# A two-block network on one Trainium2 core: modulation products placed in block one and the first FFN, high parts of weights on ScalarE, a scheduler that knows a shared port

## The chip, the core and the metric

The kernel runs on one core of a Trainium2 chip. Five engines work side by side: TensorE (PE in the profile, its weight loads PEld), VectorE (DVE), ScalarE (ACT), GpSimd (POOL) and SyncE (SP), which here only issues DMAs. The metric is the time of one execution on the device in microseconds, the median of several runs.

## The reference, cut to what matters

A token sequence of 512 x 1024 goes through two blocks in float32. Block one has two layers: a wide projection `w_in`, five kinds of attention, a gated merge, an output projection. Block two has two layers of a mixer (layer 0: convolution and mLSTM; layer 1: latent attention, MLA) and a gated convolutional FFN. In block two each layer's inputs are modulated:

```python
mod_l = jnp.split((jax.nn.silu(c) @ ada_w[layer] + ada_b[layer])[:, None, :], 6, axis=-1)
mod_c = jnp.split(jax.nn.silu(c_ctx) @ ada_w[layer] + ada_b[layer], 6, axis=-1)
h_lat = _modulate(xl, mod_l[0], mod_l[1])          # rms(x) * (1 + scale) + shift
...
xl = xl + mod_l[2] * y_lat
xl = xl + mod_l[5] * _conv_ffn(_modulate(xl, mod_l[3], mod_l[4]), ...)
```

`c` and `c_ctx` are inputs, so the modulation vectors (six vectors of 1024 for each layer and each of the two conditions) depend on nothing that the network computes. They can be made at any time before their first use.

## The kernel before, in words

Every float32 matmul is made of three: an operand is split into a high part in the type float32r and a low part, the difference, and high x high, high x low and low x high are added in PSUM (`mm3`). Activations are split when they are made. Weights are split by `wtile`: a DMA brings up to 128 x 1024 numbers into one of four `wraw` buffers, a cast writes `whi`, a subtraction writes `wlo`; both have four buffers too. In `split` the cast may go to VectorE or ScalarE (`ev`), the subtraction to VectorE or GpSimd (`tt`).

The modulation vectors don't use TensorE. `ada(l, chunks)` takes, for each chunk, four tiles of 128 rows of the transposed `ada_w` (one 512 KB DMA each, into a `wraw` buffer) and makes for each tile and condition one fused multiply-and-sum on VectorE: `ada_junk` is its unused product, `mod` the sum. A chunk is half of a vector of 1024, so a layer has twelve: 0 to 3 are shift and scale of its mixer, 4 and 5 the mixer's gate, 6 to 9 shift and scale of its FFN, 10 and 11 the FFN's gate. Layer 1 needs only its first four for the context too. That makes 160 products. Before, they stand so: layer 0's chunks 0 to 5 in block one, three in each of its layers (48 products); its other six and layer 1's chunk 0 in block two's mixer (56); chunks 1 to 6 in the first FFN (36); 7 to 11 in the MLA (20).

The order of work is written by `Plan`. Instructions are first recorded, each with a priority (its place in the code, or one that `spread` and `mix` assign between two others) and with one or more engines that could run it. `flush` then simulates the engines with a cost for each operation, gives each instruction to an engine, and emits all in the order of the simulated starts. Stages that end with a flush: block one (both layers), the mixer, the first FFN, the MLA, the second FFN.

The mixer (`mixer`) runs, in rough order: the gate projections; a depthwise convolution over 31 taps in four channel groups, each tap one instruction on VectorE that adds into `u` (120 of them, and four that begin a group), reading the padded input `apad`, of which there are two buffers; the projections of q, k, v; scans over gates; 24 units of four heads (matrices `dm`, products `ps_nd`, results `hs`); a norm of `u`; the output projection. The FFNs (`ffn`) and the output projections are long rows of matmuls. At the end of a layer of block one the last gated merge runs (`zm`: `ps_mm`, `gt`, `ps_br`, `acc`), then the merged sum is split (`mh`, `ml`) and projected with `w_out`.

Line numbers of the profile: nearly all recorded instructions have line 119, the recorder; L679 is the cast in `ev`, L695 the operation in `tt`, L690 and L691 `scale_rows`.

Of the kernel before, what the change touches and what calls it, by code (L numbers as in the profile page):

```python
# [93 lines left out]
class Op:  # L94
    __slots__ = ("i", "prio", "alts", "left", "ready", "succ", "tiles", "first", "table", "nbytes", "best", "end", "vis", "done", "nm", "why", "cols", "preds")
# [37 lines left out]
class Plan:  # L133
# [4 lines left out]
    def __init__(self, tc):  # L138
        self.tc, self.real = tc, tc.nc
        r = tc.nc  # L140
        self.tensor = PlannedEngine(self, "t", r.tensor)
        self.vector = PlannedEngine(self, "v", r.vector)
        self.scalar = PlannedEngine(self, "s", r.scalar)
        self.gpsimd = PlannedEngine(self, "g", r.gpsimd)
        self.sync = PlannedEngine(self, "y", r.sync)
        self.tile_of = {}
        self.seen = set()
        self.ops = []
        self.hist = {}
        self.kept = set()  # L150
        self.into = ()
        self.free = {e: 0.0 for e in "tsvgy"}
        self.dma_free = 0.0
        self.table = None
        self.ham = [-1, False, 0.0]
        self.released = {}
# [67 lines left out]

    def add(self, alts, name, a, k):
# [9 lines left out]
        if alts[0][0] == "t":  # L235
            dt = ins[0].dtype
            big = name != "transpose" and dt == F32
            op.cols = (4 if big else 1) * self.size(outs[0]) * ins[0].ap[0][1] / P
        op.left, op.ready, op.succ, op.done = 0, 0.0, [], False
# [131 lines left out]
    def flush(self):  # L371
# [51 lines left out]
        dma_free, table, ham = self.dma_free, self.table, self.ham  # L423
# [45 lines left out]
        while remaining:  # L469
# [22 lines left out]
            while ready[e]:  # L492
# [15 lines left out]
                if len(o.alts) > 1:  # L508
                    mine = t + o.alts[j][2] + self.LAT[e]
                    other = min((max(free[a[0]], t) + queue(a[0], p) + a[2] + self.LAT[a[0]], a[0])  # L510
                                for a in o.alts if a[0] != e)
                    if other[0] < mine:
                        heapq.heappush(pend[e], (max(free[other[1]], t + 60.0), p, i, j))
                        continue
# [35 lines left out]
            end = t + cost  # L550
# [97 lines left out]
class Net:  # L648
# [93 lines left out]
    def wtile(self, src, m, n):  # L742
# [7 lines left out]
        self.split(hv, lv, rv, m * n)  # L750
# [170 lines left out]
class BlockOne:  # L921
# [707 lines left out]
    def layer(self, l, xT):  # L1629
# [25 lines left out]
        for i, nm in enumerate(seq):  # L1655
# [16 lines left out]
            if nm == "nsa":  # L1672
                plan.spread(self.topk, self.topk[0], a0)
        for _ in self.zm(BRANCHES.index(seq[-1]), h, ys[seq[-1]], acc, False):
            pass
# [9 lines left out]
        for d, ps in n.proj_T(self.I["w_out"][l], (mh, ml), slice(0, S), D):  # L1685
# [4 lines left out]
            if l == self.layers - 1:  # L1690
                self.sums_g.add(xT[:, d], self.gain_eps[:, d:d + 1])
        return xT
# [24 lines left out]
class BlockTwo:  # L1717
# [3 lines left out]
    def beside_one(self, l, i):  # L1721

        if (l, i) == (0, 0):
            self.vecs()
            self.ada_setup()
        elif i in (1, 2, 3):
            self.ada(0, [3 * l + i - 1])
# [154 lines left out]
    def run(self, xp, xT, layers=DEPTH):  # L1882
        n, nc, tc, I = self.n, self.nc, self.tc, self.I
        self.xp = xp
        with ExitStack() as ctx:
# [4 lines left out]
            with ExitStack() as c2:  # L1890
                wk, pp = n.plan.pool(c2, "b2m"), n.plan.pool(c2, "b2mp", PSUM)
                n.wk, n.nt2 = wk, 6
                a = len(n.plan.ops)
                xT, xc = self.mixer(xT, xc, h, wk, pp)
                b = len(n.plan.ops)
                self.ada(0, range(6, 12))
                n.plan.spread((b, len(n.plan.ops)), self.begun, 0.3 * a + 0.7 * b)
                self.ada(1, [0])
# [3 lines left out]
            h = self.ffn(0, h, xT, xc, lambda: self.ada(1, range(1, 6)),  # L1902
                         lambda: (self.ada(1, [6]), self.normed("h_mla", 1, 0, xT, xc), self.weights_mla())[1])
# [19 lines left out]
    def mixer(self, xT, xc, h, wk, pp):  # L1923
# [66 lines left out]
        for half in range(2):  # L1990
            o = 2048 + 264 * half
            for t, ps in n.proj(w[:, o:o + 264], h, 264, range(6)):
                if (half, t) == (0, 0):
                    first = len(n.plan.ops)
                if (half, t) == (0, 3):
                    n.plan.spread(late, first, len(n.plan.ops))
                    self.begun = len(n.plan.ops)
# [271 lines left out]
    def mla(self, h, xT):  # L2269
        n, nc, tc, I = self.n, self.nc, self.tc, self.I  # L2270
        LAT, CTX = self.LAT, self.CTX
        with ExitStack() as ctx:
# [191 lines left out]
            a = len(n.plan.ops)  # L2464
            self.ada(1, range(7, 11))
            n.plan.spread((a, len(n.plan.ops)), 0.5 * first + 0.5 * a, 0.1 * first + 0.9 * a)
            self.ada(1, [11])
# [61 lines left out]
```

## Time and profile before

| | |
|---|---|
| median of 3 runs | 3292.95 us (3288.82 to 3294.26) |
| profiled execution, its own time | 3291.55 us |
| its span, first to last instruction | 3289.8 us |
| mean granted clock of TensorE | 0.97 |
| DMA, mean over the span | 88 GB/s |

A busy time is the time in which an engine ran at least one instruction; the granted clock is the share of the full TensorE clock that the chip allowed (1.00 is 2.4 GHz). Stage borders in the span, read from the first and last instructions on tiles of each stage: block one's layers from 0 to 784 and from 784 to 1512 us, the mixer to 1936, the first FFN to 2500, the MLA to 2905, the second FFN and the output to the end.

### The profile page before, as it was taken

The page shows a single profiled execution, that of the slowest core. Times are in us where ns is not written, and L with a number is a line of the kernel's source. Part 1 is how long each engine was busy: PE and PEld are TensorE (multiplying, and loading weights), DVE is VectorE, ACT ScalarE, POOL GpSimd, SP SyncE. Part 2 cuts the span into 40 slices and gives each one's busy share as a digit, 9 for nine tenths or more (in the row PEclk, how much of TensorE's full clock was granted, in tenths as well). Part 3 has the DMA queues.
Part 4 walks back from the last instruction along what each step waited for, and adds up shares of the span by engine and source line. Part 5 has one row for each costly group of instructions (what it writes and reads, how often), then busy time and mean ns, then how long its engine had stood idle before and what let it go on. Part 6 is the DMA issues. An engine that isn't in the chain of part 4 may idle for free.

```text
span 3289.8 us, 43893 instructions
## 1 busy us (share of the span) xinstructions
PE 3081.8 (94%) x16488; PEld 2520.2 (77%) x16488; DVE 2391.8 (73%) x4762; ACT 1177.7 (36%) x2633; POOL 325.1 (10%) x281
## 2 busy tenths in 40 slices
PE   7999898998999898998896999999998999989999
PEld 6778776877777677877775878888887777668887
DVE  8787787656887887657999775555557878766654
ACT  5444434312434434314215631111115666631112
POOL 3110110011110100010221000000001101110000
PEclk8999899999999999999997999999999999989999
DMA  5442242234332332334222223223223102133322
GB/s 183 109 112 76 63 117 68 80 93 138 85 99 80 101 88 75 81 90 154 83 77 75 74 87 94 77 69 93 78 61 96 49 20 79 46 101 106 106 76 88
DMA packets 384813, 290.01 MB, mean 88 GB/s; under 512 B 13260, under 2 KB 353496, under 8 KB 384344
## 3 DMA queue, kind: packets, MB, share of 16 engines
q1 hardware_dynamic: 384600, 287.20, 30.1%
q8 instruction: 130, 2.13, 0.3%
q14 instruction: 83, 0.68, 0.1%
HBM read 268.67 MB, written 11.67 MB: 85 GB/s over the span
## 4 chain that ended last, share of the span: by engine, by line
PE 40%; DVE 10%; ACT 1%; issue 1%; DMA 1%; POOL 0%; ACTq 0%; DVEq 0%; POOLq 0%; SPq 0%
PE ps_mm L119 32%; DVE u L119 4%; PE ps_lg L119 2%; PE ps_tp L119 2%; PE ps_pv L119 2%; DVE ada_junk L119 1%; DVE y_mod L119 1%; PE ps_nd L119 1%; PE ps_st L119 1%; DVE dm L119 0%; DVE h_ffn L119 0%; DMA wraw<-in_ab_w_in_dram 0%; DVE sq L119 0%; DMA wraw<-in_ffn_w_in_dram 0%; DVE xT L119 0%
## 5 line engine op out<-in xcount | busy, mean ns | idle before, releaser
L119 PE MATMUL ps_mm<-h_ffn,whi 128*128 128x512 f32 (+1 forms) x2112 | 567.1, 357 | 14.7 <-DVE h_ffn L119 6.9
L679 DVE CAST whi<-wraw 128x1024 fp32r<-128x1024 f32 (+7 forms) x317 | 185.3, 585 | 453.8 <-PE ps_mm L119 441.5
L119 PEld LDWEIGHTS ps_mm<-h_ffn,whi 128*128 128x128 f32 x2112 | 375.9, 190 | 77.8 <-DVE h_ffn L119 10.4
L695 DVE TENSOR_TENSOR wlo<-wraw,whi 128x1024 fp32r<-128x1024 f32 (+4 forms) x359 | 379.1, 1056 | 21.3 <-ACT whi L679 9.5
L119 PE MATMUL ps_mm<-hh,wlo 128*128 128x512 f32 x960 | 389.2, 405 | 0.2 <-DVE wlo L695 0.2
L119 PE MATMUL ps_mm<-hl,whi 128*128 128x512 f32 x960 | 388.7, 405 | 0.0
L119 PE MATMUL ps_mm<-hh,whi 128*128 128x512 f32 x960 | 387.4, 403 | 0.0
L119 PE MATMUL ps_mm<-h_ffn,wlo 128*128 128x512 f32 (+1 forms) x1056 | 375.0, 355 | 0.0
L695 POOL TENSOR_TENSOR wlo<-wraw,whi 128x1024 fp32r<-128x1024 f32 (+6 forms) x102 | 187.4, 1839 | 1099.6 <-DVE whi L679 572.9
L119 DVE CUSTOM_DVE_ANT_0 ada_junk<-wraw,cond,cols 128x1024 bf16<-128x1024 f32 x160 | 216.8, 1355 | 19.3 <-DMA wraw<-in_ada_wT_dram 18.0
L119 PEld LDWEIGHTS ps_mm<-h_ffn,wlo 128*128 128x128 f32 x1056 | 200.6, 190 | 27.7
L679 ACT CAST whi<-wraw 128x1024 fp32r<-128x1024 f32 (+8 forms) x144 | 135.8, 944 | 227.1 <-PE ps_mm L119 161.2
L119 PEld LDWEIGHTS ps_mm<-hl,whi 128*128 128x128 f32 x960 | 182.7, 190 | 34.4
L119 PEld LDWEIGHTS ps_mm<-hh,wlo 128*128 128x128 f32 x960 | 182.4, 190 | 34.0 <-DVE wlo L695 0.6
L119 PEld LDWEIGHTS ps_mm<-hh,whi 128*128 128x128 f32 x960 | 182.6, 190 | 33.6 <-issue 1.2
L119 ACT ACTIVATE p<-ps_lg,mx 128x384 f32<-128x384 f32 (+3 forms) x288 | 155.7, 544 | 129.2 <-DVE mx L119 127.1
L119 PE MATMUL ps_mm<-fhi,wlo 128*128 128x512 f32 (+1 forms) x528 | 187.8, 357 | 0.0
L119 PE MATMUL ps_mm<-flo,whi 128*128 128x512 f32 (+1 forms) x528 | 187.1, 356 | 0.0
L119 PE MATMUL ps_mm<-fhi,whi 128*128 128x512 f32 (+1 forms) x528 | 186.8, 355 | 0.0
L679 ACT COPY gpad<-ps_mm 128x512 f32<-128x512 f32 (+1 forms) x63 | 32.8, 520 | 399.7 <-PE ps_mm L119 399.0
L119 DVE TENSOR_REDUCE mx<-ps_lg 128x1 f32<-128x384 f32 (+3 forms) x288 | 144.9, 505 | 28.6 <-PE ps_lg L119 26.6
L119 PE MATMUL ps_tp<-ident,p 128*128 128x128 f32 x768 | 133.3, 278 | 12.3 <-ACT p L691 5.9
(567 smaller groups left out, 6662.0 us busy)
## 6 DMA issues: line engine op xcount, KB each, us to landing
wraw<-in_w_in_dram SPq DMA_DIRECT2D x132, 512.0 KB
wraw<-in_ada_wT_dram SPq DMA_DIRECT2D x96, 512.0 KB
wraw<-in_ffn_w_in_dram SPq DMA_DIRECT2D x88, 512.0 KB
wraw<-in_ffn_w_out_dram SPq DMA_DIRECT2D x64, 256.0 KB
wraw<-in_w_branch_dram SPq DMA_DIRECT2D x20, 512.0 KB
wraw<-in_w_out_dram SPq DMA_DIRECT2D x16, 512.0 KB
wraw<-in_ab_w_in_dram SPq DMA_DIRECT2D x16, 512.0 KB
x_keep<-xT SPq DMA_DIRECT2D x3, 2048.0 KB
```

The lines of the kernel that those rows point to most:

```text
L119: return plan.add([(eng, lambda: fn(*a, **k))], name, a, k)
L679: self.plan.either("tensor_copy", {"v": lambda x: x.tensor_copy(out, in_), "s": lambda x: x.copy(out, in_)}, out, in_)
L695: f = lambda x: x.tensor_tensor(out, a, b, op=op)
```

## The change

Three things. The products: block one keeps three chunks beside the attention of each layer and gets three more at each layer's end (`fill(l, 5)`), so that all of layer 0's are made there; all twelve of layer 1's are recorded beside the first FFN; the mixer and the MLA have none. The cast of `wtile` is recorded for ScalarE alone; the subtraction may still go to VectorE or GpSimd. And `flush` simulates a port that VectorE and GpSimd share: an instruction with two large SBUF inputs, or a copy or scaling from SBUF to SBUF (`shares`), starts on one of the two engines only when the other's last such instruction has ended.

```diff
+    def shares(self, name, outs, ins):
+        big = [x for x in ins if self.size(x) > 1 and not self.in_psum(x)]
+        if len(big) > 1:
+            return True
+        return name in ("tensor_copy", "tensor_scalar", "scale") and len(big) == 1 and not self.in_psum(outs[0])
...
-                    mine = t + o.alts[j][2] + self.LAT[e]
-                    other = min((max(free[a[0]], t) + queue(a[0], p) + a[2] + self.LAT[a[0]], a[0])
+                    start = lambda x, at: max(at, port["v"]) if x == "g" else max(at, port["g"]) if x == "v" and o.port else at
+                    mine = start(e, t) + o.alts[j][2] + self.LAT[e]
+                    other = min((start(a[0], max(free[a[0]], t)) + queue(a[0], p) + a[2] + self.LAT[a[0]], a[0])
...
-            end = t + cost
+            begin = t
+            if e == "v" and o.port:
+                begin = max(t, port["g"])
+                port["v"] = begin + cost
+            elif e == "g" and o.port:
+                begin = max(t, port["v"])
+                port["g"] = begin + cost
+            end = begin + cost
...
-        self.split(hv, lv, rv, m * n)
+        self.nc.scalar.copy(hv, rv)
+        self.tt(lv, rv, hv.bitcast(F32), ALU.subtract, m * n)
...
+        if self.fill:
+            a = len(plan.ops)
+            self.fill(l, 5)
+            plan.spread((a, len(plan.ops)), tail + 0.1 * (a - tail), tail + 0.9 * (a - tail))
...
         elif i in (1, 2, 3):
-            self.ada(0, [3 * l + i - 1])
+            self.ada(0, [6 * l + i - 1])
+        elif i == 5:
+            self.ada(0, range(6 * l + 3, 6 * l + 6))
...
-                self.ada(0, range(6, 12))
-                n.plan.spread((b, len(n.plan.ops)), self.begun, 0.3 * a + 0.7 * b)
-                self.ada(1, [0])
...
-            h = self.ffn(0, h, xT, xc, lambda: self.ada(1, range(1, 6)),
-                         lambda: (self.ada(1, [6]), self.normed("h_mla", 1, 0, xT, xc), self.weights_mla())[1])
+            h = self.ffn(0, h, xT, xc, lambda: self.ada(1, range(12)),
+                         lambda: (self.normed("h_mla", 1, 0, xT, xc), self.weights_mla())[0])
...
-            self.ada(1, range(7, 11))
-            n.plan.spread((a, len(n.plan.ops)), 0.5 * first + 0.5 * a, 0.1 * first + 0.9 * a)
-            self.ada(1, [11])
```

How the built programs' orders differ at three places. First VectorE in the mixer, where the last taps (`u`) run before the heads' first `dm`; `ISA ada_junk` is a modulation product and `ISA mod` the instruction that reads out its sum. Before:

```order
L119 SCALAR_TENSOR_TENSOR u<-apad,cw,u 128x783 x6
L119 ISA ada_junk,mod<-wraw,cond,cols 128x1024
L119 ISA mod 128x1
L119 SCALAR_TENSOR_TENSOR u<-apad,cw,u 128x783
L119 ISA ada_junk,mod<-wraw,cond,cols 128x1024
L119 ISA mod 128x1
L119 SCALAR_TENSOR_TENSOR u<-apad,cw,u 128x783
L119 ISA ada_junk,mod<-wraw,cond,cols 128x1024
L119 ISA mod 128x1
L119 SCALAR_TENSOR_TENSOR u<-apad,cw,u 128x783
L119 TENSOR_TENSOR dm<-ps_mb,u 128x128
```

The same place in the changed kernel:

```order
L119 SCALAR_TENSOR_TENSOR u<-apad,cw,u 128x783
L119 TENSOR_SCALAR u<-apad,cw,cols 128x783
L119 SCALAR_TENSOR_TENSOR u<-apad,cw,u 128x783 x7
L712 TENSOR_TENSOR wlo<-wraw,whi 128x1024
L119 SCALAR_TENSOR_TENSOR u<-apad,cw,u 128x783 x12
L119 TENSOR_TENSOR dm<-ps_mb,u 128x128
```

No product stands among the taps any more; a low part that GpSimd or nobody made there stands among them now (three in this stretch).

Second VectorE near the end of block one's first layer, in the last gated merge. Before:

```order
L679 CAST whi<-wraw 128x1024
L695 TENSOR_TENSOR wlo<-wraw,whi 128x1024
L119 SCALAR_TENSOR_TENSOR gt<-gt,ps_br 128x512
L695 TENSOR_TENSOR acc<-acc,gt 128x512
L679 CAST whi<-wraw 128x1024
L695 TENSOR_TENSOR wlo<-wraw,whi 128x1024
```

In the changed kernel:

```order
L712 TENSOR_TENSOR wlo<-wraw,whi 128x1024
L119 SCALAR_TENSOR_TENSOR gt<-gt,ps_br 128x512
L712 TENSOR_TENSOR acc<-acc,gt 128x512
L119 ISA ada_junk,mod<-wraw,cond,cols 128x1024
L119 ISA mod 128x1
L119 ISA ada_junk,mod<-wraw,cond,cols 128x1024
L119 ISA mod 128x1
L712 TENSOR_TENSOR wlo<-wraw,whi 128x1024
```

The casts have left VectorE and pairs of products (one for each condition) have come in, 24 in each layer's end.

Third VectorE at the end of the MLA, where the sums of squares (`sq`) end and the modulated input of the second FFN (`y_mod`, `h_ffn`) begins. Before:

```order
L119 TENSOR_TENSOR sq<-sq 128x512
L119 ISA ada_junk,mod<-wraw,cond,cols 128x1024
L119 ISA mod 128x1
L119 ISA ada_junk,mod<-wraw,cond,cols 128x1024
L119 ISA mod 128x1
L119 ISA ada_junk,mod<-wraw,cond,cols 128x1024
L119 ISA mod 128x1
L119 SCALAR_TENSOR_TENSOR y_mod<-xT,mod,rstd 128x512 x3
```

In the changed kernel:

```order
L119 TENSOR_TENSOR sq<-sq 128x512
L119 SCALAR_TENSOR_TENSOR xT<-ps_mm,mod,xT 128x512
L119 TENSOR_TENSOR sq<-sq 128x512
L712 TENSOR_TENSOR wlo<-wraw,whi 128x1024
L119 SCALAR_TENSOR_TENSOR y_mod<-xT,mod,rstd 128x512 x3
```

Three products are gone there, and one of the four low parts that GpSimd made for the second FFN's first weights is on VectorE.

## Rows read from the trace of the kernel before

**Rows 1.** The page, part 1: busy us, share of the span, instructions.

```profile
PE 3081.8 (94%) x16488; PEld 2520.2 (77%) x16488; DVE 2391.8 (73%) x4762; ACT 1177.7 (36%) x2633; POOL 325.1 (10%) x281
```

**Rows 2.** Busy times by stage: window, engines' busy us (instructions), granted clock, DMA share, GB/s.

```profile
0.00:784.00 784.00, 721.48 (x3736) 585.51 (x3736) 587.26 (x1255) 305.50 (x642) 106.37 (x86) 0.97 0.36 102
784.00:1512.00 728.00, 677.50 (x3489) 547.01 (x3490) 547.33 (x1148) 278.36 (x585) 75.99 (x55) 0.98 0.32 90
1512.00:1936.00 424.00, 366.20 (x2103) 314.27 (x2101) 379.09 (x657) 163.68 (x426) 62.16 (x39) 0.91 0.31 95
1936.00:2500.00 564.00, 557.31 (x3176) 485.99 (x3176) 337.15 (x523) 105.34 (x159) 17.17 (x21) 1.00 0.28 84
2500.00:2905.00 405.00, 386.64 (x2371) 283.85 (x2370) 316.75 (x866) 251.43 (x716) 47.10 (x63) 0.98 0.17 52
2905.00:3290.00 385.00, 372.65 (x1616) 303.59 (x1616) 224.22 (x317) 73.43 (x109) 16.26 (x17) 0.97 0.32 94
```

**Rows 3.** The chain that ended last, shares of the span by line.

```profile
by line: PE ps_mm L119 31.9%; DVE u L119 4.2%; PE ps_lg L119 2.3%; PE ps_tp L119 2.0%; PE ps_pv L119 1.8%; issue 1.3%; DVE ada_junk L119 1.2%; DVE y_mod L119 0.8%; PE ps_nd L119 0.8%; PE ps_st L119 0.6%; DVE dm L119 0.4%; DVE h_ffn L119 0.4
```

**Rows 4.** Busy times in the mixer's stretches and at the second FFN's entry.

```profile
1563.00:1760.00 197.00, 163.31 (x844) 137.97 (x843) 196.70 (x228) 41.21 (x86) 37.15 (x15) 0.88 0.25 75
1760.00:1880.00 120.00, 106.16 (x684) 90.90 (x683) 100.33 (x294) 82.56 (x268) 17.46 (x10) 0.89 0.24 75
1880.00:1936.00 56.00, 54.09 (x309) 46.93 (x307) 37.37 (x58) 12.64 (x22) 0.00 (x0) 1.00 0.36 109
2895.00:2922.00 27.00, 14.10 (x26) 7.82 (x27) 24.98 (x27) 12.39 (x17) 10.97 (x10) 0.56 0.58 154
```

**Rows 5.** Busy times of `ada_junk` on VectorE alone, same columns: VectorE, clock, DMA.

```profile
1563.00:1760.00 197.00, 32.80 (x24) 0.88 0.25 75
1760.00:1880.00 120.00, 20.24 (x14) 0.89 0.24 75
1936.00:2500.00 564.00, 48.70 (x36) 1.00 0.28 84
```

**Rows 6.** Groups of TensorE, 1563 to 1760: busy us, mean ns, idle before and releaser.

```profile
L119 PE MATMUL ps_mm<-wlo,h 128*128 128x512 f32 x48 | 20.1, 420 | 3.3 <-POOL wlo L695 3.3
L119 PE MATMUL ps_nd<-mv,dm 128*128 128x129 f32 x12 | 3.7, 462 | 9.3 <-DVE dm L119 9.3
```

**Rows 7.** Groups of instructions over the whole span, shapes apart, same columns.

```profile
L119 DVE CUSTOM_DVE_ANT_0 ada_junk<-wraw,cond,cols 128x1024 bf16<-128x1024 f32 x160 | 216.8, 1355 | 19.3 <-DMA wraw<-in_ada_wT_dram 18.0
L679 DVE CAST whi<-wraw 128x1024 fp32r<-128x1024 f32 x188 | 130.6, 695 | 279.7 <-PE ps_mm L119 269.3 <-issue 5.2 <-DMA wraw<-in_w_in_dram 2.0
L679 ACT CAST whi<-wraw 128x1024 fp32r<-128x1024 f32 x108 | 113.2, 1049 | 187.5 <-PE ps_mm L119 126.6 <-DMA wraw<-in_ab_w_in_dram 41.2 <-DMA wraw<-in_w_in_dram 6.8
L695 DVE TENSOR_TENSOR wlo<-wraw,whi 128x1024 fp32r<-128x1024 f32 x245 | 298.6, 1219 | 13.4 <-ACT whi L679 4.3 <-PE ps_mm L119 0.3
L695 POOL TENSOR_TENSOR wlo<-wraw,whi 128x1024 fp32r<-128x1024 f32 x51 | 132.0, 2591 | 446.0 <-ACT whi L679 268.9 <-DVE whi L679 132.8 <-PE ps_tp L119 17.2
L119 DVE SCALAR_TENSOR_TENSOR u<-apad,cw,u 128x783 f32<-128x783 f32 x120 | 139.4, 1194 | 0.2
L119 PE MATMUL ps_mm<-hh,wlo 128*128 128x512 f32 x960 | 389.2, 405 | 0.2 <-DVE wlo L695 0.2
```

**Rows 8.** The tile `apad`, 1563 to 1760: durations in ns, smallest, median, largest.

```profile
L119 DVE SCALAR_TENSOR_TENSOR u<-apad,cw,u x120: 1017/1029/3191, 1564.4 to 1757.6; 128x783 f32<-128x783 f32 x120
```

**Rows 9.** Timeline at the second FFN's entry: start us, us, engine and instruction.

```profile
2907.62 7.88 POOL L695 TENSOR_TENSOR wlo<-wraw,whi 128x1024 fp32r<-128x1024 f32 x3 [5.31 <-ACT whi L679]
2910.46 5.59 DVE L119 SCALAR_TENSOR_TENSOR y_mod<-xT,mod,rstd 128x512 f32<-128x512 f32 x2
2915.98 0.74 DVE L119 SCALAR_TENSOR_TENSOR h_ffn<-y_mod,mod,h_ffn 128x512 fp32r<-128x512 f32 x1
```

**Rows 10.** Busy times in block one's attention and at its first layer's end.

```profile
300.00:360.00 60.00, 52.99 (x292) 43.31 (x292) 58.94 (x120) 34.41 (x51) 14.54 (x14) 0.99 0.25 73
580.00:735.00 155.00, 152.71 (x716) 122.66 (x715) 96.04 (x160) 39.77 (x85) 11.06 (x5) 1.00 0.31 84
```

More of the change, by code (lines that the diff above doesn't have):

```diff
@@ L94 @@
 class Op:
-    __slots__ = ("i", "prio", "alts", "left", "ready", "succ", "tiles", "first", "table", "nbytes", "best", "end", "vis", "done", "nm", "why", "cols", "preds")
+    __slots__ = ("i", "prio", "alts", "left", "ready", "succ", "tiles", "first", "table", "nbytes", "best", "end", "vis", "done", "nm", "why", "cols", "preds", "port")
 class PlannedPool:
@@ L155, in __init__ @@
         self.ham = [-1, False, 0.0]
+        self.port = {"v": 0.0, "g": 0.0}
         self.released = {}
@@ L238, in add @@
             op.cols = (4 if big else 1) * self.size(outs[0]) * ins[0].ap[0][1] / P
+        op.port = self.shares(name, outs, ins)
         op.left, op.ready, op.succ, op.done = 0, 0.0, [], False
@@ L422, in flush @@
         frontier = 0
-        dma_free, table, ham = self.dma_free, self.table, self.ham
+        dma_free, table, ham, port = self.dma_free, self.table, self.ham, self.port
         order = []
@@ L1673, in layer @@
                 plan.spread(self.topk, self.topk[0], a0)
+        tail = a0
         for _ in self.zm(BRANCHES.index(seq[-1]), h, ys[seq[-1]], acc, False):
@@ L1892, in run @@
                 n.wk, n.nt2 = wk, 6
-                a = len(n.plan.ops)
                 xT, xc = self.mixer(xT, xc, h, wk, pp)
-                b = len(n.plan.ops)
-                self.ada(0, range(6, 12))
-                n.plan.spread((b, len(n.plan.ops)), self.begun, 0.3 * a + 0.7 * b)
-                self.ada(1, [0])
                 h = self.normed("h_ffn", 0, 3, xT, xc)
@@ L1996, in mixer @@
                     n.plan.spread(late, first, len(n.plan.ops))
-                    self.begun = len(n.plan.ops)
                 nog = 264 if half == 0 else 248
@@ L2463, in mla @@
             out(3, y2)
-            a = len(n.plan.ops)
-            self.ada(1, range(7, 11))
-            n.plan.spread((a, len(n.plan.ops)), 0.5 * first + 0.5 * a, 0.1 * first + 0.9 * a)
-            self.ada(1, [11])
             h = self.normed("h_ffn", 1, 3, xT, None)
```

## Prediction, made before the changed kernel was run

> **What bounds the kernel now.** I read the view by engine first, then the same busy times cut at the stage borders, then the chain of work that ended last, and only then single instructions. TensorE (PE) is busy 94% of the span and VectorE (DVE) 73% [rows 1], and an average over six stages says little. Cut by stage [rows 2], the two FFNs leave TensorE almost nothing to win (557.31 us busy of 564, 372.65 of 385). The mixer of block two is the odd one: TensorE 366.20 of 424 us at a granted clock of 0.91, and VectorE 379.09 of 424, the only stage in which VectorE is busier than TensorE. Block one's two layers lie between: TensorE idles 62.5 and 50.5 us there.
>
> The chain says what that means [rows 3]: 4.2% of the span is the line of `u` (the convolution's taps) and 1.2%, some 39 us, is `ada_junk`, the modulation product. An instruction that only prepares numbers for later stands on the path that sets the end.
>
> Where it stands there is seen by cutting the mixer [rows 4]. From 1563 to 1760 VectorE is busy 196.70 of 197 us, while TensorE idles 34 us and is granted 0.88 of its clock. From 1760 to 1880 (the heads) VectorE has 100.33 of 120, TensorE 106.16 at 0.89, ScalarE (ACT) 82.56. From 1880 to 1936 TensorE has 54.09 of 56: bound by matmuls again. The products take 32.80 us (24 of them) of the first stretch and 20.24 us (14) of the second [rows 5]. TensorE's waits in the first name VectorE (9.3 us for `dm` alone), and 3.3 us go to a low part that GpSimd (POOL) makes [rows 6].
>
> **The change part by part.** *Products out of the mixer.* 56 of 160 leave the mixer and 20 leave the attention stage; 48 more go into the ends of block one's layers, 28 more into the first FFN. One takes 1.355 us on VectorE [rows 7].
>
> Taps' stretch, 1563 to 1760: VectorE is the bound, so the 32.80 us come off whole, unless something else is late. The order shows three low parts (`wlo`) among the taps on VectorE where there were none, 3 x 1.219 us [rows 7] = 3.7 us back. The casts don't count here: the mixer's were on ScalarE already but for six. Net 29; I take 28, for a POOL part more or less. The bounds: TensorE's 163.31 us in this stretch, at 0.88 of the clock, must still fit into 169. If neither its clock rises nor its other waits fall, little more than half is won, so -15. At the other end, the taps' excess over their median, 120 x (1194 - 1029) ns = 20 us [rows 7, 8], could go too: -48. What is late next: the scans behind the gates and GpSimd's low parts, which stay.
>
> Heads, 1760 to 1880: 20.24 us of products leave a VectorE that is 84% busy, beside a TensorE that idles 13.8 us. Nothing is won if TensorE and ScalarE pace the units, 20 if VectorE does. TensorE waits on `dm`, `hs` and `den` made by VectorE, and its idle time is the nearest measure: -12.
>
> Out-projection, 1880 to 1936: TensorE fills it [rows 4], so whatever leaves VectorE there was hidden: 0.
>
> *Entry of the second FFN.* From 2895 to 2922 TensorE has 14.10 of 27 us at 0.56 of the clock [rows 4]. VectorE there makes `y_mod` and `h_ffn`, 16 operations that take 0.74 us alone, but two `y_mod` took 5.59 us, just while three low parts ran on GpSimd for 7.88 us [rows 9]. Three products stand right before them. In the new order the products are gone, ScalarE casts these tiles ahead of `rstd`, and GpSimd's three (one less than before) can run earlier, beside the out-projection's sums. From 0 (they meet the `sq` sums instead) to -8 (twice that pair's excess of 4.1 us, for what else they held up); I take -5.
>
> *Products into block one's ends.* 24 more in each layer, 24 x 1.355 = 32.5 us. From 580 to 735 TensorE has 152.71 of 155, VectorE 96.04 [rows 10]. With the products it has 128.5, still 83%, less the casts that leave. The cover is the 59 us in which VectorE idles while TensorE multiplies; all 24 end before `mh` in the order, so the hand-over to the out-projection is not touched. Each product also brings a 512 KB DMA on SP's queue, through the four `wraw` slots that the weights use; DMA engines are 31% busy there. I take 0. The bound comes from 300 to 360 [rows 10]: VectorE at 58.94 of 60, TensorE at 52.99. If the ends became like that, 12% of 155 us in each layer would be lost, +36.
>
> *Products into the first FFN.* 36 become 64: 38 us more for a VectorE that idles 227 of 564 [rows 2]; 36 of them (48.70 us, [rows 5]) run there today beside a TensorE at 99%. 0. Without that cover they would cost the 38.
>
> *High parts on ScalarE.* All casts of weights on VectorE (the 188 widest alone are 130.6 us, 0.695 each) go to ScalarE, at 1.049 [rows 7]. ScalarE is busy 36% [rows 1]. The chain DMA, cast, subtract, matmul grows by 0.35 us for a tile, behind four buffers of each kind; TensorE's 960 matmuls with the low part in block one waited 0.2 us for it in all [rows 7]. So 0 on this side; the bound is 0.354 us for each of block one's 123 casts that move (by the order), +44. On the other side VectorE is relieved: in block one 123 casts leave, but the order puts 12 low parts, 11 `acc` sums and some smaller operations of GpSimd on it instead, about half of that. If a tenth of block one's 113 us of idle TensorE went, -11. I take 0 between.
>
> *The scheduler's port model* costs no instruction. It moves work from GpSimd (286 instructions in the program become 205) to VectorE, so its price is in the figures above.
>
> Sum: -28 - 12 - 5 = -45 us. The profiled execution took 3291.55 us, 1.75 more than its span, and lies 1.4 below the median of the runs, inside their spread. 3291.55 - 45 = 3246.5, so 3246.
>
> **Weighed against a rule.** The taps' median is 1.029 us and their longest 3.191 [rows 8]; a low part on GpSimd takes 2.591 [rows 7]: a tap can stand for most of one. The Trainium skill (SBUF — State Buffer, "Who interferes with whom") says that a DVE operation with two SBUF inputs and a GpSimd operation that reads SBUF take turns on one port pair, and that the one that comes second is blocked for the whole of the other. By that rule a scheduler that knows it could get rid of all of the excess; the sum would be -65 and the time 3226. The trace agrees with the blocking (taps of either 1.03 or up to 3.19 us); whether the plan avoids it is the first rival.
>
> **The rivals.** *The excess goes too.* If GpSimd's low parts in the mixer no longer meet the taps, the 20 us of excess go with the 45: 3226. For it: the planner now charges either engine for the other's time. Against: the order still has 16 low parts on GpSimd in the mixer (18 before), and the taps stand in a row with hardly anything between them that could run beside one. With a gain in block one as above, 3215.
>
> *TensorE takes VectorE's place in the mixer.* If the clock stays at 0.88 and the heads are paced by TensorE and ScalarE, -15, 0 and -5 are left: 3272. For it: 163.31 of 169 us would be nearly full. Against: the clock fell where TensorE starved (0.88 here against 1.00 in the first FFN).
>
> *Slower: the casts hold TensorE in block one.* There ScalarE also makes the exponentials and evictions on which attention waits; a cast of 1.049 us in front of one delays it. The 123 casts that move decide it: at 0.37 us of TensorE each the 45 us are gone, at 0.45 the kernel is slower by 10, 3302. For it: TensorE and VectorE are both near their limits in stretches like 300 to 360. Against: ScalarE has 34 of 60 us there, and the low parts were on time everywhere.
>
> *No change.* The taps could wait for matmuls instead of the products; then the mixer stays and only -5 is left, 3287. Against: VectorE idled 0.3 us in 197.
>
> **How the numbers follow.** Forecast (25 to 60 us faster) 0.60, own range 3231 to 3267; the excess goes too 0.12; TensorE takes the place 0.13; about no change 0.05; slower, through casts or the block's ends, 0.10. About 0.2%, 6.6 us, is what a measurement of this kernel can tell from no change: faster 0.85, same 0.05, slower 0.10. The range reaches from 3212 (just under the first rival with block one's gain) to 3282; that leaves out the slower cases, the unchanged one and the far end of the first rival, 0.18 to 0.2 in all.
>
> **What the profile would show.** Right: the mixer down from 424 to about 384 us, no `ada_junk` in it, the granted clock between the taps' start and the heads' end above 0.9, `ada_junk` gone from the chain or under 0.3%, the `u` share as it was; ends of block one still over 97% TensorE; first FFN 564 +- 3. Wrong: taps still without a gap and the stretch as long as before (something else fills VectorE); TensorE idle behind `whi` or `wlo` in block one (the casts); layers longer than 784 and 728 us with idle time before `ps_br` or `ps_mm` in their ends (the products or their DMAs).

## The result, and the profile after

The changed kernel took 3250.5 us (median of 4 runs, 3245.89 to 3252.26) where the kernel before took 3292.7: a ratio of 0.9871, 95% interval [0.9855, 0.9887]. The forecast was 3246. The profiled execution took 3249.24 us, its span 3247.5. The page of the changed kernel, by engine as in [rows 1]:

```profile
PE 3069.0 (95%) x16488; PEld 2518.3 (78%) x16488; DVE 2294.8 (71%) x4602; ACT 1396.0 (43%) x2874; POOL 204.4 (6%) x200
```

The busy times of the changed kernel by stage, cut where its own stages end, to be read against [rows 2]:

```profile
0.00:784.00 784.00, 722.83 (x3738) 588.30 (x3738) 589.95 (x1270) 366.33 (x708) 56.85 (x61) 0.97 0.39 112
784.00:1502.00 718.00, 675.14 (x3480) 549.06 (x3481) 540.97 (x1154) 326.36 (x634) 40.13 (x34) 0.97 0.35 97
1502.00:1900.00 398.00, 355.33 (x2110) 308.20 (x2108) 313.67 (x547) 170.46 (x435) 57.43 (x33) 0.94 0.22 64
1900.00:2469.00 569.00, 558.60 (x3177) 486.11 (x3178) 353.66 (x544) 153.75 (x210) 11.38 (x13) 1.00 0.35 105
2469.00:2872.00 403.00, 387.81 (x2370) 284.55 (x2369) 294.77 (x820) 260.07 (x730) 38.30 (x53) 0.98 0.12 35
2872.00:3247.00 375.00, 369.33 (x1616) 302.05 (x1616) 201.75 (x271) 119.01 (x161) 0.27 (x6) 0.99 0.30 87
```

The gain is where it was looked for. VectorE in the mixer went from 379.09 us to 313.67, so TensorE, with 355.33, is the busier engine there now as it is in the other stages, at a clock of 0.94 where it had 0.91. The two stretches of the mixer that were costed and the out-projection, as in [rows 4] (180, 94 and 65 us long):

```profile
1561.00:1741.00 180.00, 157.79 (x874) 137.37 (x872) 173.43 (x187) 44.44 (x94) 46.84 (x17) 0.92 0.19 53
1741.00:1835.00 94.00, 88.16 (x624) 76.69 (x625) 75.28 (x251) 75.42 (x253) 4.00 (x3) 0.98 0.08 24
1835.00:1900.00 65.00, 61.87 (x341) 52.75 (x339) 30.08 (x49) 20.37 (x35) 0.00 (x0) 0.97 0.24 76
```

For comparison between kernels, the stages below are cut at the same events in every trace: block one ends with the last matmul of its second output projection; the mixer (with its entry) and the MLA end with the first matmul on `h_ffn`; the first FFN ends with the first on `h_mla`; the last column is the second FFN and the output.

| us | block one | mixer | first FFN | MLA | second FFN, output |
|---|---|---|---|---|---|
| before | 1509.4 | 426.8 | 566.4 | 402.4 | 384.7 |
| after | 1502.4 | 398.0 | 568.2 | 403.8 | 375.1 |

So -7.0, -28.8, +1.8, +1.4 and -9.6: the span is 42.3 us shorter. Inside the mixer, from the first tap to the last, 195.0 us became 180.0; from there to the last `ps_nd` 113.1 became 93.3; and the wait between block one and the first matmul on the context, 5.9 us before, is 11.3 now.

The taps' stretch has 173.43 us of VectorE in 180, so VectorE is still its busiest engine, though no longer without a gap. Groups of VectorE and GpSimd there in the changed kernel, shapes apart (busy us, mean ns, idle before and releaser):

```profile
L119 DVE SCALAR_TENSOR_TENSOR u<-apad,cw,u 128x783 f32<-128x783 f32 x120 | 134.6, 1158 | 0.6
L119 DVE SCALAR_TENSOR_TENSOR og<-og,hg 128x512 f32<-128x512 f32 x6 | 8.3, 1392 | 0.0
L119 DVE TENSOR_TENSOR_SCAN b<-ones,lf 4x768 f32<-4x768 f32 x1 | 3.9, 3941 | 0.0
L119 DVE TENSOR_TENSOR_SCAN M<-ones,M,li 4x512 f32<-4x512 f32 x1 | 3.3, 3297 | 0.0
L712 POOL TENSOR_TENSOR wlo<-wraw,whi 128x1024 fp32r<-128x1024 f32 x15 | 45.5, 3044 | 127.1 <-ACT whi L119 127.1
```

and the two groups of the kernel before that they are read against, the sums `og` and GpSimd's wide low parts in its taps' stretch (the first two scans above took 1.737 and 1.274 us there):

```profile
L119 DVE SCALAR_TENSOR_TENSOR og<-og,hg 128x512 f32<-128x512 f32 x6 | 4.0, 685 | 0.0
L695 POOL TENSOR_TENSOR wlo<-wraw,whi 128x1024 fp32r<-128x1024 f32 x12 | 34.0, 2833 | 79.6 <-ACT whi L679 78.8 <-DVE u L119 0.8
```

The taps' excess did not go: 120 x (1158 - 1027) ns = 15.7 us is left of 20 (their smallest, median and longest below, as in [rows 8]), and `og` and two scans now have long ones too. GpSimd's wide low parts in the stretch rose from 12 to 15, from 34.0 to 45.5 us.

```profile
L119 DVE SCALAR_TENSOR_TENSOR u<-apad,cw,u x120: 1018/1027/3192, 1562.6 to 1740.1; 128x783 f32<-128x783 f32 x120
```

TensorE's longest wait in the stretch, by group, is a new one: a projection can't go on until `apad` of the next channel group is written (3.4 us before, at one place):

```profile
L119 PE MATMUL ps_mm<-whi,h 128*128 128x512 f32 x96 | 31.7, 411 | 12.5 <-DVE apad L119 12.5
```

At the second FFN's entry, the 27 us that answer to [rows 4] and one line of the timeline that answers to [rows 9]: TensorE has 20.38 us at 0.75 of the clock instead of 14.10 at 0.56, GpSimd 3.30 instead of 10.97, and three `y_mod` take 2.08 us where two took 5.59.

```profile
2862.00:2889.00 27.00, 20.38 (x67) 14.36 (x68) 20.07 (x26) 13.41 (x18) 3.30 (x8) 0.75 0.26 75
...
2870.84 2.08 DVE L119 SCALAR_TENSOR_TENSOR y_mod<-xT,mod,rstd 128x512 f32<-128x512 f32 x3 [4.12 <-ACT rstd L119]
```

### The profile page after: what moved, and what is told of

Same layout as the page of the kernel before. It is cut to its first block, busy times and chain, and to the rows that moved or that the text cites. A ratio compares the mean times of both kernels' runs of the same rounds, so it can differ in the third digit from the quotient of the medians.

```text
span 3247.5 us, 44054 instructions
## 1 busy us (share of the span) xinstructions
PE 3069.0 (95%) x16488; PEld 2518.3 (78%) x16488; DVE 2294.8 (71%) x4602; ACT 1396.0 (43%) x2874; POOL 204.4 (6%) x200
## 4 chain that ended last, share of the span: by engine, by line
PE 51%; DVE 8%; DMA 3%; ACT 3%; issue 1%; ACTq 0%; DVEq 0%; SPq 0%
PE ps_mm L119 40%; PE ps_lg L119 3%; PE ps_tp L119 3%; DMA wraw<-in_ada_wT_dram 3%; PE ps_pv L119 2%; DVE u L119 2%; PE ps_br L119 1%; PE ps_nd L119 1%; DVE wlo L712 1%; DVE ada_junk L119 1%; DVE y_mod L119 1%; PE ps_st L119 0%; ACT dm L119 0%; PE ps_ss L119 0%; DVE sq L119 0%
## 5 line engine op out<-in xcount | busy, mean ns | idle before, releaser
L119 ACT CAST whi<-wraw 128x1024 fp32r<-128x1024 f32 (+8 forms) x461 | 408.9, 889 | 838.3 <-PE ps_mm L119 778.9
L712 DVE TENSOR_TENSOR wlo<-wraw,whi 128x1024 fp32r<-128x1024 f32 (+5 forms) x386 | 401.0, 1041 | 141.5 <-ACT whi L119 137.3
L119 DVE CUSTOM_DVE_ANT_0 ada_junk<-wraw,cond,cols 128x1024 bf16<-128x1024 f32 x160 | 209.3, 1308 | 115.9 <-DMA wraw<-in_ada_wT_dram 114.4
L712 POOL TENSOR_TENSOR wlo<-wraw,whi 128x1024 fp32r<-128x1024 f32 (+3 forms) x75 | 148.2, 1981 | 856.1 <-ACT whi L119 756.1
L119 DVE SCALAR_TENSOR_TENSOR xT<-ps_mm,mod,xT 128x512 f32<-128x512 f32 x136 | 101.8, 749 | 93.5 <-PE ps_mm L119 93.1
L119 PEld LDWEIGHTS ps_tp<-ident,p 128*128 128x128 f32 x768 | 93.2, 142 | 55.3 <-ACT p L708 20.2
```

Source lines behind the costliest of these rows:

```text
L119: return plan.add([(eng, lambda: fn(*a, **k))], name, a, k)
L712: f = lambda x: x.tensor_tensor(out, a, b, op=op)
```

## The experiments

First each part alone, then the pairs, then two questions that the result left: what GpSimd's low parts cost in the mixer, and what the products cost in block one. Ratios are to the kernel before, timed on the same chip, with 95% intervals.

**Each part alone.** Products moved, as in the diff of the change, and nothing else:

> The kernel before with the products moved and nothing else: casts on either engine, the scheduler without the port. Theory (the move of the products alone carries the gain, the other two parts are worth nothing): mixer 424 to about 387 us, entry of the second FFN 5 shorter, block one no longer than before; 3247 to 3258 us. Rival (the products in block one's ends are only free because the casts left VectorE): each end of a layer is longer by 5 to 18 us, 3262 to 3285 us. Rival (the scheduler's port is what keeps the taps free): mixer shorter by 25 or less, about 3268 us.

Casts on ScalarE alone:

```diff
-        self.split(hv, lv, rv, m * n)
+        self.nc.scalar.copy(hv, rv)
+        self.tt(lv, rv, hv.bitcast(F32), ALU.subtract, m * n)
```

> The kernel before with the casts of weights on ScalarE alone: products and scheduler as before. Theory (casts are worth nothing by themselves except the late context load at the mixer's entry): block one within 5 us of before, the wait for the context tiles 5 us longer, the rest as before; 3290 to 3300 us. Rival (relieving VectorE is a gain by itself, the 7 us that block one lost in the changed kernel come from it): 3280 to 3288 us. Rival (casts hold TensorE in block one): 3300 us or more.

The port in the scheduler alone (`shares`, `start` and `begin` of the change):

> The kernel before with the shared port in the scheduler and nothing else. It moves 6 low parts between engines over the whole program. Theory (no price of its own): 3286 to 3298 us, the taps' mean above their median as before (165 ns). Rival (a scheduler that knows the port keeps low parts away from taps): taps' mean under 1.09 us, mixer shorter by 10 us or more, about 3280 us.

**The pairs.** The changed kernel without the port, without the cast's line, and with the products where they were:

> The changed kernel without the shared port in the scheduler: products moved and casts on ScalarE. Theory (casts and products belong together: casts off VectorE make room in block one's ends for the products, and the port adds nothing): 3242 to 3254 us, block one as in the changed kernel. Rival (the parts simply add, -23 and +3): 3270 to 3276 us, so the port would have brought 20 in company where it cost 15 alone. Rival (the port costs 15 in company too): about 3236 us.

> The changed kernel with the casts on either engine again: products moved and port known. Theory (the casts make the room for the products in block one, 13 us with and without the port): block one 10 to 18 us longer than in the changed kernel, 3260 to 3272 us. Rival (the port costs 15 wherever the casts may go to VectorE, as it did alone): the products' 23 less 15, 3280 to 3290 us.

> The kernel before with casts on ScalarE and the port known, products as before. Theory (with the casts fixed the port gains some 6 us in block one, and the mixer stays as it was): block one some 17 us shorter than before, 3283 to 3292 us. Rival (the port sends more low parts to GpSimd in the mixer and costs there what it wins in block one): 3293 to 3302 us.

Measured, with the stages of the profiled executions (the kernels before and after again, to have all eight together):

| products moved | casts on ScalarE | port | median us | ratio | block one | mixer | rest |
|---|---|---|---|---|---|---|---|
| - | - | - | 3293 | 1 | 1509.4 | 426.8 | 1353.6 |
| yes | - | - | 3270.42 | 0.9925 [0.9912, 0.9937] | 1526.3 | 394.2 | 1348.1 |
| - | yes | - | 3296.49 | 1.0007 [0.9999, 1.0016] | 1501.6 | 433.5 | 1357.3 |
| - | - | yes | 3308.12 | 1.0036 [1.0024, 1.0049] | 1519.9 | 439.0 | 1347.4 |
| yes | yes | - | 3256.24 | 0.9886 [0.9872, 0.9901] | 1513.1 | 391.5 | 1347.4 |
| yes | - | yes | 3257.22 | 0.9885 [0.987, 0.99] | 1516.3 | 392.1 | 1344.9 |
| - | yes | yes | 3282.83 | 0.9965 [0.9952, 0.9978] | 1501.3 | 429.4 | 1347.4 |
| yes | yes | yes | 3250.5 | 0.9871 [0.9855, 0.9887] | 1502.4 | 398.0 | 1347.1 |

Against what was expected:

- Products alone: the theory failed and the first rival held (3270.42 us, block one 16.9 us longer).
- Casts alone: the theory's time held, but block one is 7.8 us shorter and not within 5.
- Port alone: both readings failed. The kernel is slower than either range, and the taps' mean is 1.221 us where it was 1.194.
- Without the port: all three failed. Block one is 10.7 us longer than in the changed kernel, the mixer 6.5 us shorter.
- Without the casts' line: block one is 13.9 us longer, as the theory had it, but the time lies 2.8 us under its range, since the mixer is 5.9 us shorter.
- With the products where they were: the time is within 0.2 us of the theory's range, but block one is 8.1 us shorter than before and not 17.

Four things stand in the table. Moving the products shortens the mixer in every company, by 32.6, 42.0, 46.9 and 31.4 us (row against row with the same casts and port). In block one the same move costs 16.9 us alone and 11.5 beside the casts, but with the port -3.6, and with both 1.1. Moving the casts shortens block one in every company, by 7.8, 13.2, 18.6 and 13.9 us. The port shortens it where the products have been moved (by 10.0, and 10.7 beside the casts); where they have not, it makes it 10.5 us longer, or leaves it as it was beside the casts. And the parts don't add: by the medians -23, +3 and +15 alone would make -5 (by the ratios -25, +2 and +12, so -10), together they are -42. Since a scheduler writes a new order for each of these kernels, differences of some 5 us in one stage are not to be read as the price of a part.

Where the products hurt block one when they are moved alone is seen at its first layer's end, where [rows 10] had TensorE busy for 152.71 of 155 us. The kernel of that run, the window of its end and the whole of block one:

```profile
580.00:744.00 164.00, 156.97 (x718) 125.03 (x716) 119.45 (x189) 46.83 (x97) 17.98 (x9) 0.98 0.40 114
...
0.00:1526.00 1526.00, 1404.53 (x7218) 1138.81 (x7219) 1184.23 (x2468) 595.03 (x1244) 195.94 (x147) 0.97 0.37 103
```

VectorE has 119.45 of 164 us there, by its share not full, yet TensorE idles 7 us, with waits of 2.0 and 2.6 us at the start of the stretch for `p` scaled on GpSimd and on ScalarE, and its clock is 0.98 instead of 1.00. The 96 products of block one take 1.356 us each on average in that run, the longest 3.344, and 1.288 in the changed kernel, the longest 1.786: that is 6.6 us of VectorE. What makes up the rest of the 16.9 us was not taken apart.

**GpSimd's low parts in the mixer.** The changed kernel with the mixer's low parts on VectorE (`low_v` is set while the mixer is recorded):

```diff
-        self.tt(lv, rv, hv.bitcast(F32), ALU.subtract, m * n)
+        if self.low_v:
+            self.nc.vector.tensor_tensor(lv, rv, hv.bitcast(F32), op=ALU.subtract)
+        else:
+            self.tt(lv, rv, hv.bitcast(F32), ALU.subtract, m * n)
```

> The changed kernel with the mixer's 16 low parts of weights that GpSimd makes put on VectorE. Theory (a low part on GpSimd blocks the VectorE instruction beside it for nearly all of its 2.6 us, so 1.2 us on VectorE itself is cheaper): the taps all take 1.03 us, the six sums og 0.69, the scans lose their 2 us; VectorE has 16 x 1.2 = 19 us more and some 25 less; mixer 2 to 10 us shorter, 3241 to 3248 us. Rival (the blocking is partial or lies beside other waits): VectorE's stretch grows by the 16 low parts, mixer 5 to 18 us longer, 3255 to 3268 us.

Measured: 3235.23 us, 0.9824 [0.981, 0.9837], 15 us faster than the changed kernel and beyond the theory's range; the mixer is 16.4 us shorter (381.6). Its taps' stretch, 160 us long, with the groups that answer to those above and the taps' durations:

```profile
1559.00:1719.00 160.00, 149.63 (x840) 128.33 (x838) 158.62 (x190) 40.94 (x77) 0.74 (x1) 0.97 0.19 53
...
L119 DVE SCALAR_TENSOR_TENSOR u<-apad,cw,u 128x783 f32<-128x783 f32 x120 | 120.6, 1029 | 1.2
L119 DVE TENSOR_TENSOR wlo<-wraw,whi 128x1024 fp32r<-128x1024 f32 x14 | 17.0, 1217 | 0.0
L119 DVE SCALAR_TENSOR_TENSOR og<-og,hg 128x512 f32<-128x512 f32 x6 | 4.1, 681 | 0.0
...
L119 DVE TENSOR_TENSOR_SCAN b<-ones,lf 4x768 f32<-4x768 f32 x1 | 1.7, 1739 | 0.0
L119 DVE TENSOR_TENSOR_SCAN M<-ones,M,li 4x512 f32<-4x512 f32 x1 | 1.3, 1273 | 0.0
...
L119 DVE SCALAR_TENSOR_TENSOR u<-apad,cw,u x120: 1018/1029/1037, 1560.3 to 1717.8; 128x783 f32<-128x783 f32 x120
```

Not one of 120 taps is longer than 1.037 us. VectorE has 13 more wide low parts and yet 14.8 us less to do. Taps, `og` and the two scans alone are 134.6 + 8.3 + 3.9 + 3.3 - 120.6 - 4.1 - 1.7 - 1.3 = 22.4 us shorter, so each of GpSimd's 15 cost VectorE about 1.5 us or more (a third scan, 3.292 us in the changed kernel and 1.274 here, is not counted), where VectorE makes one in 1.217. The clock rose from 0.92 to 0.97 and the wait for `apad` is gone. The stretch lost 20 us; the heads behind it took 9 back (102.4 where the changed kernel had 93.3).

The next kernel adds casts on either engine for the three tiles that block one fetches ahead for the mixer (`cast_v` is set around `prefetch` in `weights_mixer`), for the 5.4 us by which the wait ahead of the context tile had grown:

```diff
-        self.nc.scalar.copy(hv, rv)
+        if self.cast_v:
+            self.ev(hv, rv, m * n)
+        else:
+            self.nc.scalar.copy(hv, rv)
```

> The changed kernel with the mixer's low parts on VectorE and, besides, the casts of the three weight tiles that are fetched ahead for the mixer on either engine, as before the change. Theory (ScalarE's cast behind the norms holds a buffer that the context tile waits for): the wait before the context tile falls from 11.3 to about 6 us, 3228 to 3231 us. Rival (the wait ends with something else, or is given back): as without it, 3233 to 3237 us.

Measured: 3236.88 us, 0.9826 [0.9813, 0.9839], the same as without it. Windows of the wait and of the stretch to the first tap, first without the edit, then with it:

```profile
1504.50:1515.70 11.20, 3.57 (x10) 1.20 (x9) 5.40 (x11) 7.73 (x12) 0.90 (x4) 0.76 0.22 71
1515.70:1558.80 43.10, 40.93 (x264) 37.35 (x265) 28.44 (x56) 22.67 (x44) 2.91 (x9) 0.94 0.62 187
```

```profile
1503.00:1508.90 5.90, 3.51 (x9) 1.13 (x8) 2.50 (x4) 5.03 (x8) 0.90 (x4) 1.00 0.28 89
1508.90:1558.20 49.30, 43.15 (x264) 38.49 (x265) 32.50 (x62) 23.47 (x46) 3.09 (x9) 0.90 0.56 169
```

The wait fell to 5.9 us as expected, and the stretch behind it grew by 6.2: TensorE's waits for `h` from ScalarE are 5.0 us there instead of 1.2. The context was early, the other tokens were not, so the wait was no loss of its own.

Then the low parts on VectorE everywhere, and the same without the port:

```diff
-    low_v = False
+    low_v = True
```

> As the run before it, with the low parts of weights on VectorE everywhere: 27 in block one, 4 in the first FFN and 28 in the MLA leave GpSimd too. Theory (a low part on GpSimd costs VectorE more than one made on VectorE, in every stage): 2 to 10 us faster than the run before it, 3219 to 3228 us. Rival (outside the mixer VectorE is not the bound, and TensorE waits longer for low parts that queue on VectorE): the same or up to 12 us slower, 3230 to 3242 us.

```diff
-        op.port = self.shares(name, outs, ins)
+        op.port = False
...
-                    start = lambda x, at: max(at, port["v"]) if x == "g" else max(at, port["g"]) if x == "v" and o.port else at
+                    start = lambda x, at: at
```

> The run with all low parts on VectorE, without the port in the scheduler. Theory (once no low part is on GpSimd, there is next to nothing left for the port to decide): within 4 us of that run, 3223 to 3231 us. Rival (what the port wins in block one is in other operations, the sums and small products of attention): 6 to 14 us slower, 3233 to 3241 us.

Measured: 3226.98 us, 0.9794 [0.9781, 0.9808], the fastest of these kernels, and without the port 3241.79, 0.9842 [0.9827, 0.9856]. For the first run the theory held, 10 us, of which the MLA has 4 (399.8 us instead of 403.8). For the second it failed: 15 us are lost, all in block one (1516.9 against 1501.6), since low parts are not all that the port decides; the rival had the direction, and its range ends 0.8 us below. Block one in both, first with the port, then without it, with GpSimd's sums `acc`:

```profile
0.00:1501.00 1501.00, 1399.01 (x7208) 1138.04 (x7217) 1140.49 (x2454) 692.61 (x1340) 34.67 (x65) 0.96 0.37 105
...
L714 POOL TENSOR_TENSOR acc<-acc,gt 128x512 f32<-128x512 f32 x2 | 2.6, 1290 | 29.8 <-DVE gt L119 29.8
```

```profile
0.00:1517.00 1517.00, 1404.63 (x7219) 1133.70 (x7220) 1133.60 (x2393) 696.22 (x1350) 116.86 (x117) 0.97 0.37 104
...
L714 POOL TENSOR_TENSOR acc<-acc,gt 128x512 f32<-128x512 f32 x21 | 43.5, 2071 | 437.1 <-DVE gt L119 384.0 <-DVE sm L119 35.3 <-DMA wraw<-in_ada_wT_dram 17.8
```

With the port GpSimd is busy 82 us less in block one, and VectorE, which does most of that work instead, only 7 us longer.

**Products in block one.** The 48 products of the ends made beside the attention instead:

```diff
-            self.ada(0, [6 * l + i - 1])
-        elif i == 5:
-            self.ada(0, range(6 * l + 3, 6 * l + 6))
+            self.ada(0, [6 * l + i - 1, 6 * l + i + 2])
```

> The changed kernel with the 48 products of block one's ends made beside the attention instead (two chunks where there was one). Theory (the ends are the better cover: VectorE is near its limit in attention): block one 10 to 36 us longer, 3260 to 3286 us. Rival (any place in block one is cover enough now that the casts are gone): within 4 us of the changed kernel, about 3250 us.

Measured: 3288.4 us, 0.9976 [0.9966, 0.9986]: four fifths of the gain are gone, 36.7 us of it in block one (1539.1 us). The theory had the direction, and the loss lies just past its range; the rival failed. In its first layer's attention, 400 to 580 us, VectorE has 149.51 of 180 us and TensorE 155.56 at a clock of 0.91; first the same part of the changed kernel, 164.45 of 177 us at 0.96, then this one:

```profile
400.00:577.00 177.00, 164.45 (x933) 134.06 (x934) 140.34 (x340) 83.06 (x184) 4.69 (x11) 0.96 0.36 102
400.00:580.00 180.00, 155.56 (x867) 123.16 (x865) 149.51 (x353) 83.44 (x191) 16.84 (x18) 0.91 0.39 109
```

And without these 48 products (zeros stand in their `mod`):

```diff
-        elif i == 5:
-            self.ada(0, range(6 * l + 3, 6 * l + 6))
...
+        for o in (12, 36):
+            nc.gpsimd.memset(self.mod[0][:, o:o + 12], 0.0)
```

> The changed kernel without the 48 products in block one's ends: layer 0's chunks 3 to 5 and 9 to 11 are zeros instead. Theory (they cost what the comparison of the runs without the port gives, 1513 against 1502 us to the end of block one): block one 8 to 14 us shorter, 3236 to 3243 us. Rival (they are hidden behind TensorE, as predicted): block one within 3 us, 3247 to 3252 us. Rival (they cost as much as without the casts' move, 17): about 3233 us.

Measured: 3248.68 us, 0.9856 [0.984, 0.9872]; block one 1503.1 us with nothing to make in its ends, 1502.4 with 48 products. The theory is wrong and the first rival right: in the changed kernel the products cost nothing there that can be measured. The first layer's end, in the changed kernel and then without them:

```profile
577.00:732.00 155.00, 153.00 (x712) 121.82 (x711) 105.34 (x179) 58.50 (x108) 1.38 (x1) 1.00 0.42 121
580.00:737.00 157.00, 156.45 (x732) 126.33 (x731) 84.69 (x144) 57.55 (x103) 3.63 (x2) 1.00 0.31 85
```

## Why the prediction was right, step by step

**Taps' stretch, -28 (bounds -15 and -48): -15.0.** The mechanism was right and the size wrong. That it came out on the lower bound is chance: the bound was worked out from a TensorE at 0.88 of its clock, and TensorE has 157.79 of 180 us at 0.92. All 24 products are gone (32.80 us, [rows 5]), and the three low parts came back as foretold. Mis-sized was "a POOL part more or less": GpSimd has 15 low parts there, all wide, where it had 13; the taps' excess fell by 4.8 us, but `og` and two scans take 8.4 us more than they do alone. And VectorE stood still for 6.6 us: 3.4 before a copy of `mk`, for a TensorE that had no gap just then, and 2.4 before a `dm`, for ScalarE. Where one or both of the other two parts were left out, the moved products gave 172.4 to 173.9 us, -21 to -23, with longer heads (97.0 to 103.5): how the gain is cut between taps and heads belongs to the order, and only their sum is to be read. The bound of -48 was not a fancy: with GpSimd's low parts gone from the mixer the stretch is 160 us, -35, with the low parts' own 17 us in it.

**Heads, -12 (0 to -20): -19.8**, the far end. TensorE idles 5.8 us there instead of 13.8 and its clock is 0.98 instead of 0.89 (windows above and [rows 4]). That the step priced TensorE's idle time alone was its error: the clock came back with it. Cut exactly from the last tap to the last `ps_nd`, TensorE idles 6.7 us less and is busy 13.1 us less (652 matmuls in 100.73 us at 0.88, now 622 in 87.66 at 0.98). At the mean of before, 30 matmuls are some 4.6 us, the shifted border; by this estimate the other 8.4 are matmuls that run faster. Both stretches together were to give -40 and gave -34.8.

**The clock.** "The clock fell where TensorE starved" held: between the taps' start and the heads' end it was over 0.9, so that the rival in which TensorE takes VectorE's place failed: its -15 for the taps was measured, but not its clock of 0.88, and the heads gave 19.8 us where it had 0.

**Entry of the second FFN, -5 (0 to -8): -9.6, or -8.2 with the MLA's end, 1.4 us later now.** Right in mechanism, too small. With the products moved alone the last column falls by 9.3 us already (375.4 against 384.7), so it needed neither the casts nor the port (the port alone takes 5.9 us off that column, the casts alone nothing). The sums `sq` meet GpSimd's low parts now, as the step's upper end had it (the last two took 2.2 us each), and it was worth it.

**Products into block one's ends, 0 (bound +36).** True in the changed kernel, as the run without them shows, and for a reason that the step did not have: "the cover is the 59 us in which VectorE idles" was not enough by itself. Moved alone, the products cost block one 16.9 us. With the port but not the casts' line block one takes 1516.3 us, with the casts' line but not the port 1513.1, and only with both 1502.4. That the ends are the right place and attention is not was right: 36.7 us were lost when they were put there. That this is the bound's +36 is chance, since the bound was 12% of the ends' own time.

**High parts on ScalarE, 0 (+44 to -11).** Right for the whole time when it stands alone (1.0007 [0.9999, 1.0016]), but not for block one: there the casts' move is worth 7.8 us alone, and 13.2 to 18.6 in company, beyond the -11 that "a tenth of the 113 us" allowed. The longer wait for the context tile, which the step missed, cost nothing, as the run that removed it shows. The slower rival, casts that hold TensorE in block one, did not happen.

**The scheduler's port, "no own cost".** Wrong as a statement on the part: alone it makes the kernel slower by 0.36%, in the whole it brings some 6 us (0.9886 to 0.9871, intervals that overlap), and where all low parts are on VectorE 15 us. Beside the other two parts it won 10.7 us in block one, where it takes sums and scalings off GpSimd. That this is the reason is not shown: without the moved products it takes them off as well (`acc` on GpSimd falls from 13 to 2, beside the casts from 16 to 2), and block one gains nothing (10.5 us longer alone, 0.3 shorter beside the casts). It lost in the mixer (391.5 to 398.0). Its order puts 16 of the mixer's low parts on GpSimd there instead of 12, but of the 6.5 us taps and heads together have only 0.9; 4.2 stand before the first tap and 1.4 in the out-projection. In the code it compares what each engine would need for the low part itself, and VectorE's own next instruction, which the low part holds up, is in neither figure. Why the port alone loses 10 us in block one and 12 in the mixer was not taken apart either.

**First FFN, 564 +- 3**: cut at the events it went from 566.4 to 568.2, so 1.8 us longer, right. Of the other signs, the mixer has no `ada_junk`, and block one's first end is still 98.7% TensorE (153.00 of 155 us); but the mixer, which was to be 40 us shorter, is 28.8. **The chain** was foretold wrong in two points. `u` was to stay at 4.2% and is at 1.7%; `ada_junk` was to go and is at 0.6%, beside 2.6% of waits for its DMA, most of them in the first FFN:

```profile
by line: PE ps_mm L119 40.4%; PE ps_lg L119 2.9%; PE ps_tp L119 2.6%; DMA wraw<-in_ada_wT_dram 2.6%; PE ps_pv L119 2.4%; DVE u L119 1.7%; issue 1.4%; PE ps_br L119 1.1%; PE ps_nd L119 0.8%; DVE wlo L712 0.6%; DVE ada_junk L119 0.6%; DVE y_m
```

That costs next to nothing (TensorE is busy 558.60 of 569 us there): a chain runs through an engine's queue wherever that queue was the last to be ready, by however little.

So the sum of -45 came out as -42 with terms that missed in both directions: the taps gave 13 less than foretold, the heads 8 more, the entry of the second FFN 5 more and block one 7 more; the mixer's entry and out-projection, priced at nothing, took 6, the first FFN and the MLA 3. That the sum comes so near is in part luck. The rival "the excess goes too" did not happen, but what it spoke of, VectorE's waits beside GpSimd's low parts, is the largest thing that was still to be had: with no low part of a weight on GpSimd 0.9871 became 0.9794.

## What to carry to other kernels

Where an engine bounds a stage, take what is only preparation out of it, and put it where another engine is the bound; but try the move alone as well as in company, since here the same 48 instructions cost 17 us or none, depending on what else was changed with them. Work that is given to a slower engine "for nothing" has to be priced by what it holds up, not by its own end: GpSimd's low parts cost VectorE more than making them. A wait that grew is a loss only if the work behind it was ready: test it by removing it.

## What the runs showed of the hardware

The Trainium skill (SBUF — State Buffer, "Who interferes with whom") says that a VectorE operation with two SBUF inputs and a GpSimd operation that reads SBUF exclude each other for the whole of the one that came first; the runs agree, and show a price that was not expected. In the changed kernel a low part runs on GpSimd from 1578.27 to 1580.77 us, and a tap that starts at 1578.77 ends at 1581.60, after 2.83 us instead of 1.03. The lock takes a scan of 1.274 us or a tiny `den` (two columns, 0.151 alone) just as well as a tap of 1.029: in the changed kernel they are seen at 3.297 and at a mean of 1.228, and the busy time of VectorE in the profile contains the waiting. This fits the 82 us that could leave GpSimd in block one for 7 us more of VectorE. GpSimd waits too: one low part takes 6.18 us while five taps run through beside it at 1.02, and the `acc` sums take 1.290 us each where two are left and 2.071 where there are 21.
